# Placing four mixing steps one group later, and giving the operand loads of the merges a pool of their own

## The chip, the cores and the metric

The kernel runs on one core of one Trainium2 chip. Its time is device microseconds of one execution of the whole program; a run before and after are compared by the median of several executions. One execution is taken with the hardware profiler, and every row shown below is from that one. The engines are named as in the profile: PE is TensorE (PEld its weight loads), DVE VectorE, ACT ScalarE, POOL GpSimd, SP the sync engine, which here issues all the DMA transfers.

## The reference

A single layer with two parallel branches: stick-breaking attention, and a pooling branch that works at four window lengths.

```python
WINDOWS = (2, 4, 8, 16)                  # four groups of 256 channels
hs = concat(meta, x)                      # 16 + 1024 tokens of 2048
h = rmsnorm(hs, gain)
q, k, v, g_attn, u, g_pool, m_attn, m_pool = split(h @ w_in)
o_attn = stick_breaking_attention(q, k, v) * silu(g_attn)
pooled[g] = mean of u[g] over the last WINDOWS[g] tokens - u[g]
mixed[g] = pooled[g] @ pool_w[g]          # 256 x 256 for each group
o_pool = mixed * pool_scale * silu(g_pool)
merged = sigmoid(m_attn) * (o_attn @ w_attn_up) + sigmoid(m_pool) * (o_pool @ w_pool_up)
out = rmsnorm(hs + merged @ w_out, final_gain)[meta:]
```

The change touches the mixing of pooled channels (`mixed`) and the beginning of the merges (`o_pool @ w_pool_up`).

## The kernel before

All matrix products are in fp32 with three matmuls for one (`mm3`, L137 to L140): an operand is split into a high part h and a low part l, and h x h, h x l and l x h are added up in PSUM. A split is one activation on ACT (L116, writes the high part) and one subtraction, mostly on DVE, for some weights on POOL (L117, writes the low part). So each matrix that is loaded goes through SP (the load), ACT and DVE or POOL before PE can use it. The weights go through three rings of four buffers: `wr` (as loaded, L124), `wh` and `wl` (split).

The large products are done by block products with fewer multiplications, in stages:

* Up to about 985 us: the norm and the first products of the blocks, whose results go to DRAM.
* Phase 2 (L545 to L883): the rest of the products. `duo` (L572 to L622) computes two columns of blocks of 128 channels with three sub-steps, m5, n4 and p3, each with sixteen weight blocks of 128 by 128 and evacuations on DVE (L592, L594). It runs first for the gates of the pooling groups 0 to 2, then for the pooling (L675 to L714), then for the attention heads one by one (`kv`, `gq`, and two gates of the merges after each).
* The merges (L885 to L977): 32 chunks of 48 matmuls each, sixteen for each of `w_pool_up` ("p") and `w_attn_up` ("a"). A chunk multiplies 128 output channels, for both halves of the tokens.
* The output product and the last norm (L979 on).

The loop over the pooling groups (L675) does four things for group g, one after the other. (1) It loads and splits `pool_w[g]` into `pwh` and `pwl`. (2) It computes the channels u of the group with `duo`. (3) For each of the two 128-channel halves (cc = 1, then 0) it forms the window sums by doubling, one addition on DVE over 1024 tokens for each doubling (L692: one for window 2, four for window 16), subtracts u (L697), and splits the result into `ph` (ACT) and `pl` (DVE). (4) It mixes: 24 matmuls of 128x512 with `pwh`/`pwl` as weights and `ph`/`pl` as moving operands into four PSUM tiles `acc`; each is scaled and gated on DVE (L713) into a tile `st` (two buffers) and stored to DRAM, `d_op` (L714, on SP). For the last group the product of its gate (`silu_duo`, "gp" 3) stands between (3) and (4). `acc` is a ring of four PSUM tiles that `duo` uses as well.

At the start of the merges the operands `d_op` (16 tiles of 128x512) and `d_oa` (16 tiles, from the attention) are loaded back into tiles `ol` (L901; six buffers, within the pool `pm` that holds all else of the merges) and split into the operands x (`op`, `oa`). The first chunk's weights are tied: `tc.issue_after` lets their loads be issued only after the sixth of the first eight operand loads (`behind`). The first two gate tiles (`first`, loads of `d_sp`) are asked for ahead of the operands. The order of the chunks is p0, p8, p1, then a0, a8 and so on in turn.

A scheduler lays out the order of each engine's instructions: it goes by the order in which the program asks for them, and by the time at which it thinks that buffers and operands come free. Each engine then works its own list in order. What a change of code does to those lists is therefore read from the lists themselves.

Of the kernel before, what the change touches and what calls it, by code (L numbers as in the profile page):

```python
# [9 lines left out]
F32 = mybir.dt.float32  # L10
# [5 lines left out]
P = 128  # L16
# [56 lines left out]
def trunk_kernel(  # L73
# [37 lines left out]
    def nm(s):  # L111
        uid[0] += 1
        return f"{s}_{uid[0]}"
# [5 lines left out]
    def load_split(hi, lo, src, eng=None):  # L119
        raw = wp.tile([P, 512], F32, tag="wr", name=nm("wr"), bufs=4)  # L120
        if len(src.shape) == 3:
            c = src.shape[2]
            raw, hi, lo = (t.rearrange("p (k c) -> p k c", c=c) for t in (raw, hi, lo))
        nc.sync.dma_start(raw, src)  # L124
        split(hi, lo, raw, eng)
# [102 lines left out]
    with ExitStack() as actx:  # L228
# [395 lines left out]
        def duo(*args):  # L624
            for call in duo_steps(*args):
                call()
# [10 lines left out]
        with ExitStack() as a0ctx:  # L637
# [33 lines left out]
            for i in (0, 2, 1):  # L671
                for calls in every:
                    calls[i]()

            for g, win in enumerate(WINDOWS):  # L675
                pwh = a0.tile([P, 512], F32R, tag="pwh", name=nm("pwh"), bufs=1)
                pwl = a0.tile([P, 512], F32R, tag="pwl", name=nm("pwl"), bufs=1)
                load_split(pwh, pwl, pool_w[g].rearrange("(c p) d -> p c d", p=P))
                pwh, pwl = (t.rearrange("p (c d) -> p c d", d=256) for t in (pwh, pwl))
                d = named["u", g]  # L680
                us = [tok_tile(a0, "u", F32) for _ in range(2)]
                nc.sync.dma_start(us[0][:, META : META + HALF], d_c[d.n])
                nc.sync.dma_start(us[0][:, :META], d_cm[d.n])
                duo(d, lambda key: half_of(us[key[0]], key[1], META), lambda key, t: None, us[1][:, :META])
                ph, pl = [None] * 2, [None] * 2
                for cc in (1, 0):
                    u = us[cc]
                    cur, lo, sh = u, 0, 1
                    while sh < win:
                        nxt = tok_tile(a0, "s", F32)  # L690
                        lo += sh
                        nc.vector.tensor_tensor(out=nxt[:, lo:], in0=cur[:, lo:], in1=cur[:, lo - sh : TOK - sh], op=ALU.add)  # L692
                        cur, sh = nxt, 2 * sh
                    pool_l = a0.tile([P, SEQ], F32R, tag="pl", name=nm("pl"))
                    pool_h = a0.tile([P, SEQ], F32R, tag="ph", name=nm("ph"))
                    raw = cur[:, META:]
                    nc.vector.scalar_tensor_tensor(out=raw, in0=cur[:, META:], scalar=1.0 / win, in1=u[:, META:], op0=ALU.mult, op1=ALU.subtract)  # L697
                    split(pool_h, pool_l, raw)
                    ph[cc], pl[cc] = pool_h, pool_l
                if g == GROUPS - 1:  # L700
                    sils.append(sil_tiles())
                    silu_duo(a0, named["gp", g], sils[g])
                sil = sils[g]
                for dc in range(2):
                    dd = slice(dc * P, (dc + 1) * P)
                    ch = 2 * g + dc
                    for i in range(2):
                        t = slice(i * 512, (i + 1) * 512)
                        a = acc_tile()
                        for n, cc in enumerate((1, 0)):  # L710
                            mm3(a, pwh[:, cc, dd], pwl[:, cc, dd], ph[cc][:, t], pl[cc][:, t], n == 0, n == 1)
                        st = a0.tile([P, 512], F32, tag="st", name=nm("st"), bufs=2)
                        nc.vector.scalar_tensor_tensor(out=st, in0=a, scalar=psc[:, ch : ch + 1], in1=sil[dc][:, t], op0=ALU.mult, op1=ALU.mult)  # L713
                        nc.sync.dma_start(d_op[ch][:, t], st)  # L714

        with tc.tile_pool(name="a1", bufs=1, side="right", reuse_waits="tile") as a1:
            MK = 64 + META
# [176 lines left out]
        q, jj = divmod(j, QD)  # L894
        split(A[q][0][:, jj], A[q][1][:, jj], src)

    with tc.tile_pool(name="pm", bufs=2, side="right", reuse_waits="tile") as pm:

        def fill(A, j, src):
            raw = pm.tile([P, 512], F32, tag="ol", name=nm("ol"), bufs=6)  # L900
            ins = nc.sync.dma_start(raw, src)  # L901
            put(A, j, raw)
            return ins
# [23 lines left out]
        for n, k in enumerate((("p", 0), ("p", KH), ("p", 1))):  # L927
            order.remove(k)
            order.insert(n, k)
        first = [gate("sp", 6, d_sp, 0, t) for t in range(2)]  # L930
        op, oa = [xquads(0, HALF, xo), xquads(1, HALF, xo)], [xquads(2, HALF), xquads(3, HALF, xc)]
        behind = [fill_up(op[t], d_op, t) for t in range(2)][0]
        sps, ms = {}, {}

        def sums(j):
# [15 lines left out]
        forms = w_forms(pm)  # L951
        for n, (kind, c) in enumerate(order):
            if n in (0, 1):
                fill_up(oa[n], d_oa, n)
            if kind == "p":
                gs = [gate("sp", 6, d_sp, c, t) for t in range(2)] if n else first
                for t, a in up_mm(w_pu, op, c, None if n else behind):
                    nc.vector.tensor_tensor(out=gs[t], in0=a, in1=gs[t], op=ALU.mult)
                sps[c] = gs
            else:  # L960
# [225 lines left out]
```

## Time and profile before

| | us |
|---|---|
| three executions | 2588.91, 2588.54, 2584.05 |
| median | 2588.54 |
| the profiled execution, its own time | 2589.82 |
| its span, first to last instruction | 2588.1 |
| PE busy in the span | 2462.5 (95%) |
| DVE, POOL, ACT busy | 1268.1, 1005.4, 896.8 |

The mean granted clock of PE over the span is 0.982 of full. A matmul of 128x512 at full clock starts 0.23 us after the one ahead of it. In rows of the timeline the columns are the start, the duration, then engine, line, operation, what it writes and reads, and in brackets the idle time ahead of it with what ended it. In rows of waits they are the total, the number of times, and the longest. Matmuls of the mixing are known by their operands `ph`, `pl`; those of the merges by their PSUM tile `accb`.

### The profile page before, as it was taken

The numbers are of one execution on the slowest core, as the hardware profiler recorded it, in microseconds if no ns is written. First come the engines' busy times: TensorE is split into PE (matmuls) and PEld (weight loads), VectorE is DVE, ScalarE is ACT, GpSimd is POOL, SyncE is SP. The second block draws the span as 40 slices with busy tenths as digits, with TensorE's granted clock in tenths as the row PEclk, the third lists the DMA queues.
The fourth block names the chain that finished last, engine by engine and source line by source line (L and its number), as shares of the span: only waits on it lengthen the run. The fifth ranks groups of instructions, "written<-read, shape, count | busy, mean of one in ns | idle before, by whom it ended". The sixth has DMA issues, their size and how long they took to land.

```text
span 2588.1 us, 35874 instructions
## 1 busy us (share of the span) xinstructions
PE 2462.5 (95%) x12680; PEld 2087.6 (81%) x12680; DVE 1268.1 (49%) x2089; ACT 896.8 (35%) x1845; POOL 1005.4 (39%) x898
## 2 busy tenths in 40 slices
PE   6899999999999999899999999999949999989998
PEld 5676778888888887888888888888748888867887
DVE  5442234553333344575676567656652322445556
ACT  6421122222222234224454455545431111144243
POOL 1655555554454544233323333333104545520212
PEclk8999999999999999999999999999979999999999
DMA  5566555665555557435334443443286777675534
GB/s 181 168 208 212 196 195 201 215 232 175 179 184 183 184 179 231 133 115 151 123 118 136 127 126 117 141 126 91 86 280 208 250 237 246 225 248 183 190 124 171
DMA packets 390516, 457.81 MB, mean 177 GB/s; under 512 B 32432, under 2 KB 234544, under 8 KB 389296
## 3 DMA queue, kind: packets, MB, share of 16 engines
q1 hardware_dynamic: 390336, 455.53, 54.7%
q8 instruction: 99, 1.62, 0.3%
q14 instruction: 81, 0.66, 0.1%
HBM read 313.11 MB, written 142.31 MB: 176 GB/s over the span
## 4 chain that ended last, share of the span: by engine, by line
PE 77%; DMA 7%; DVE 6%; POOL 3%; ACT 2%; issue 2%; SPq 0%; DVEq 0%; POOLq 0%; ACTq 0%
PE acc L138 17%; PE acc L140 17%; PE acc L139 17%; PE accb L138 4%; PE accb L139 4%; PE accb L140 4%; POOL r L270 3%; PE accb L1012 2%; PE accb L1011 2%; PE accb L1010 2%; DMA mr<-d_f 2%; DMA raw<-in_w_in_dram 2%; PE tr L764 1%; DVE s L692 1%; DVE x L117 1%
## 5 line engine op out<-in xcount | busy, mean ns | idle before, releaser
L138 PE MATMUL acc<-x,wh 128*128 128x512 f32 (+2 forms) x2736 | 980.1, 359 | 25.2 <-ACT wh L116 16.4
L140 PE MATMUL acc<-x,wl 128*128 128x512 f32 (+2 forms) x2736 | 971.1, 355 | 7.3 <-DVE wl L117 6.0
L139 PE MATMUL acc<-x,wh 128*128 128x512 f32 (+2 forms) x2736 | 968.8, 354 | 0.0
L138 PEld LDWEIGHTS acc<-x,wh 128*128 128x128 f32 x2736 | 519.4, 190 | 97.0 <-ACT wh L116 22.1
L140 PEld LDWEIGHTS acc<-x,wl 128*128 128x128 f32 x2736 | 518.3, 189 | 85.3 <-DVE wl L117 13.3
L139 PEld LDWEIGHTS acc<-x,wh 128*128 128x128 f32 x2736 | 519.4, 190 | 62.7
L116 ACT ACTIVATE wh<-wr 128x512 fp32r<-128x512 f32 x408 | 256.6, 630 | 593.7 <-PE accb L139 235.4
L117 DVE TENSOR_TENSOR wl<-wr,wh 128x512 fp32r<-128x512 f32 x288 | 221.1, 770 | 248.2 <-ACT wh L116 230.0
L117 DVE TENSOR_TENSOR wl<-r,wh 128x512 fp32r<-128x512 f32 x160 | 149.5, 938 | 345.6 <-ACT wh L116 328.5
L117 POOL TENSOR_TENSOR wl<-wr,wh 128x512 fp32r<-128x512 f32 x120 | 166.6, 1388 | 346.0 <-ACT wh L116 289.3
L116 ACT ACTIVATE wh<-r 128x512 fp32r<-128x512 f32 x160 | 100.3, 631 | 474.9 <-POOL r L270 369.6
L270 POOL TENSOR_TENSOR r<-raw,raw 128x512 f32<-128x512 f32 x80 | 111.1, 1388 | 379.2 <-DMA raw<-in_w_in_dram 348.9
L138 PE MATMUL accb<-x,wh 128*128 128x512 f32 x512 | 200.2, 391 | 32.4 <-ACT wh L116 32.4
L270 POOL TENSOR_TENSOR r<-r,raw 128x512 f32<-128x512 f32 x160 | 221.6, 1385 | 12.5 <-DMA raw<-in_w_in_dram 2.5
L139 PE MATMUL accb<-x,wh 128*128 128x512 f32 x512 | 199.9, 390 | 0.0
L140 PE MATMUL accb<-x,wl 128*128 128x512 f32 x512 | 199.7, 390 | 0.0
L1010 PE MATMUL accb<-wh,x 128*128 128x512 f32 x416 | 163.8, 394 | 7.1 <-ACT wh L116 7.0
L1012 PE MATMUL accb<-wl,x 128*128 128x512 f32 x416 | 164.2, 395 | 0.2
L1011 PE MATMUL accb<-wh,x 128*128 128x512 f32 x416 | 162.7, 391 | 0.0
L748 DVE TENSOR_TENSOR_SCAN wt<-wt 128x272 f32<-128x272 f32 (+5 forms) x128 | 107.7, 842 | 110.2 <-POOL wt L743 64.8
L117 DVE TENSOR_TENSOR wl<-raw,wh 128x512 fp32r<-128x512 f32 x136 | 102.6, 765 | 100.9 <-ACT wh L116 100.8
L116 ACT ACTIVATE wh<-raw 128x512 fp32r<-128x512 f32 x160 | 97.6, 624 | 135.2 <-PE acc L139 100.3
(176 smaller groups left out, 3059.5 us busy)
## 6 DMA issues: line engine op xcount, KB each, us to landing
raw<-in_w_in_dram SPq DMA_DIRECT2D x96, 512.0 KB, 5.8
d_r<-r SPq DMA_DIRECT2D x160, 256.0 KB, 2.0
wr<-d_r SPq DMA_DIRECT2D x160, 256.0 KB, 2.9
raw<-in_w_in_dram SPq DMA_DIRECT2D x152, 256.0 KB, 5.3
wr<-in_w_in_dram SPq DMA_DIRECT2D x80, 256.0 KB, 3.0
cw<-in_w_out_dram SPq DMA_DIRECT2D x64, 256.0 KB, 5.1
d_wf<-cw SPq DMA_DIRECT2D x64, 256.0 KB, 2.8
wr<-d_wf SPq DMA_DIRECT2D x64, 256.0 KB, 3.0
```

What stands on the lines that cost most here:

```text
L116: nc.scalar.activation(hi, src, AF.Copy)
L117: (eng or nc.vector).tensor_tensor(out=lo, in0=src, in1=hi.bitcast(F32), op=ALU.subtract)
L138: nc.tensor.matmul(ps, wh, rh, start=first, stop=False, skip_group_check=skip)
L139: nc.tensor.matmul(ps, wh, rl, start=False, stop=False, skip_group_check=skip)
L140: nc.tensor.matmul(ps, wl, rh, start=False, stop=last, skip_group_check=skip)
L270: nc.gpsimd.tensor_tensor(out=t, in0=a, in1=b, op=ALU.add)
L692: nc.vector.tensor_tensor(out=nxt[:, lo:], in0=cur[:, lo:], in1=cur[:, lo - sh : TOK - sh], op=ALU.add)
L748: nc.vector.tensor_tensor_scan(out=rev, data0=rev, data1=rev, initial=wt[:, w : w + 1], op0=ALU.mult, op1=ALU.bypass)
L764: nc.tensor.transpose(tr[:, n, :], bt[:, off : off + P], ident)
L1010: nc.tensor.matmul(a, sh, wh, start=first and j == 0, stop=False, skip_group_check=not first)
L1011: nc.tensor.matmul(a, sl, wh, start=False, stop=False, skip_group_check=not first)
L1012: nc.tensor.matmul(a, sh, wl, start=False, stop=j == KH - 1, skip_group_check=not first)
```

## The change

```diff
--- before.py
+++ after.py
@@ -672,16 +672,37 @@
                 for calls in every:
                     calls[i]()
 
+            mixed = {}
+
+            def mix_weights(g):
+                pw = [a0.tile([P, 512], F32R, tag=f"pw{m}", name=nm("pw"), bufs=1) for m in range(2)]
+                load_split(*pw, pool_w[g].rearrange("(c p) d -> p c d", p=P))
+                return [t.rearrange("p (c d) -> p c d", d=256) for t in pw]
+
+            def mix(g, pwh, pwl):
+                ph, pl = mixed.pop(g)
+                for dc in range(2):
+                    dd = slice(dc * P, (dc + 1) * P)
+                    ch = 2 * g + dc
+                    for i in range(2):
+                        t = slice(i * 512, (i + 1) * 512)
+                        a = acc_tile()
+                        for n, cc in enumerate((1, 0)):
+                            mm3(a, pwh[:, cc, dd], pwl[:, cc, dd], ph[cc][:, t], pl[cc][:, t], n == 0, n == 1)
+                        st = a0.tile([P, 512], F32, tag="st", name=nm("st"), bufs=2)
+                        nc.vector.scalar_tensor_tensor(out=st, in0=a, scalar=psc[:, ch : ch + 1], in1=sils[g][dc][:, t], op0=ALU.mult, op1=ALU.mult)
+                        nc.sync.dma_start(d_op[ch][:, t], st)
+
             for g, win in enumerate(WINDOWS):
-                pwh = a0.tile([P, 512], F32R, tag="pwh", name=nm("pwh"), bufs=1)
-                pwl = a0.tile([P, 512], F32R, tag="pwl", name=nm("pwl"), bufs=1)
-                load_split(pwh, pwl, pool_w[g].rearrange("(c p) d -> p c d", p=P))
-                pwh, pwl = (t.rearrange("p (c d) -> p c d", d=256) for t in (pwh, pwl))
+                if g:
+                    pw = mix_weights(g - 1)
                 d = named["u", g]
                 us = [tok_tile(a0, "u", F32) for _ in range(2)]
                 nc.sync.dma_start(us[0][:, META : META + HALF], d_c[d.n])
                 nc.sync.dma_start(us[0][:, :META], d_cm[d.n])
                 duo(d, lambda key: half_of(us[key[0]], key[1], META), lambda key, t: None, us[1][:, :META])
+                if g:
+                    mix(g - 1, *pw)
                 ph, pl = [None] * 2, [None] * 2
                 for cc in (1, 0):
                     u = us[cc]
@@ -697,21 +718,11 @@
                     nc.vector.scalar_tensor_tensor(out=raw, in0=cur[:, META:], scalar=1.0 / win, in1=u[:, META:], op0=ALU.mult, op1=ALU.subtract)
                     split(pool_h, pool_l, raw)
                     ph[cc], pl[cc] = pool_h, pool_l
-                if g == GROUPS - 1:
-                    sils.append(sil_tiles())
-                    silu_duo(a0, named["gp", g], sils[g])
-                sil = sils[g]
-                for dc in range(2):
-                    dd = slice(dc * P, (dc + 1) * P)
-                    ch = 2 * g + dc
-                    for i in range(2):
-                        t = slice(i * 512, (i + 1) * 512)
-                        a = acc_tile()
-                        for n, cc in enumerate((1, 0)):
-                            mm3(a, pwh[:, cc, dd], pwl[:, cc, dd], ph[cc][:, t], pl[cc][:, t], n == 0, n == 1)
-                        st = a0.tile([P, 512], F32, tag="st", name=nm("st"), bufs=2)
-                        nc.vector.scalar_tensor_tensor(out=st, in0=a, scalar=psc[:, ch : ch + 1], in1=sil[dc][:, t], op0=ALU.mult, op1=ALU.mult)
-                        nc.sync.dma_start(d_op[ch][:, t], st)
+                mixed[g] = ph, pl
+            pw = mix_weights(GROUPS - 1)
+            sils.append(sil_tiles())
+            silu_duo(a0, named["gp", GROUPS - 1], sils[-1])
+            mix(GROUPS - 1, *pw)
 
         with tc.tile_pool(name="a1", bufs=1, side="right", reuse_waits="tile") as a1:
             MK = 64 + META
@@ -894,10 +905,12 @@
         q, jj = divmod(j, QD)
         split(A[q][0][:, jj], A[q][1][:, jj], src)
 
-    with tc.tile_pool(name="pm", bufs=2, side="right", reuse_waits="tile") as pm:
+    with ExitStack() as mctx:
+        po = mctx.enter_context(tc.tile_pool(name="po", bufs=6, side="right", reuse_waits="tile"))
+        pm = mctx.enter_context(tc.tile_pool(name="pm", bufs=2, side="right", reuse_waits="tile"))
 
         def fill(A, j, src):
-            raw = pm.tile([P, 512], F32, tag="ol", name=nm("ol"), bufs=6)
+            raw = po.tile([P, 512], F32, tag="ol", name=nm("ol"))
             ins = nc.sync.dma_start(raw, src)
             put(A, j, raw)
             return ins
@@ -927,9 +940,10 @@
         for n, k in enumerate((("p", 0), ("p", KH), ("p", 1))):
             order.remove(k)
             order.insert(n, k)
-        first = [gate("sp", 6, d_sp, 0, t) for t in range(2)]
-        op, oa = [xquads(0, HALF, xo), xquads(1, HALF, xo)], [xquads(2, HALF), xquads(3, HALF, xc)]
-        behind = [fill_up(op[t], d_op, t) for t in range(2)][0]
+        op, oa = [], []
+        for t in range(2):
+            op.append(xquads(t, HALF, xo))
+            fill_up(op[t], d_op, t)
         sps, ms = {}, {}
 
         def sums(j):
@@ -951,10 +965,11 @@
         forms = w_forms(pm)
         for n, (kind, c) in enumerate(order):
             if n in (0, 1):
+                oa.append(xquads(3, HALF, xc) if n else xquads(2, HALF))
                 fill_up(oa[n], d_oa, n)
             if kind == "p":
-                gs = [gate("sp", 6, d_sp, c, t) for t in range(2)] if n else first
-                for t, a in up_mm(w_pu, op, c, None if n else behind):
+                gs = [gate("sp", 6, d_sp, c, t) for t in range(2)]
+                for t, a in up_mm(w_pu, op, c, None):
                     nc.vector.tensor_tensor(out=gs[t], in0=a, in1=gs[t], op=ALU.mult)
                 sps[c] = gs
             else:
```

In the loop over the groups the mixing (4) of group g is no longer in the turn of its own group: the mixing of group g-1, with the load of its weights, stands after `duo` of group g. The last group's mixing stays where it was, after its gate. `mix_weights` and `mix` hold the old lines, `mixed` keeps `ph` and `pl` in between, and the tiles `pwh`/`pwl` are now `pw0`/`pw1`, named `pw`.

In the merges the tiles `ol` come from a pool `po` of their own, opened ahead of `pm`. The weights of the first chunk are no longer tied to an operand load, the first two gate tiles are asked for in their turn in the loop, and the operand tiles `op` and `oa` are made just ahead of their loads.

What this makes of PE's list shows after u of group 1. Before, the last matmuls of u (into `acc_9468`, with x and wh) are followed by the mixing of the same group 1, whose `ph_9665` was made from that u:

```order
L138 MATMUL acc_9468<-x_1651_8857,wh_9631 128x256
L139 MATMUL acc_9468<-x_1652_8858,wh_9631 128x256
L140 MATMUL acc_9468<-x_1651_8857,wl_9630 128x256
L138 MATMUL acc_9678<-ph_9665,pwh_9453 128x512
L138 MATMUL acc_9688<-ph_9665,pwh_9453 128x512
L138 MATMUL acc_9698<-ph_9665,pwh_9453 128x512
L138 MATMUL acc_9708<-ph_9665,pwh_9453 128x512
L139 MATMUL acc_9678<-pl_9664,pwh_9453 128x512
L140 MATMUL acc_9678<-ph_9665,pwl_9454 128x512
```

After, the same u (now `acc_9422`) is followed by the mixing of group 0, whose `ph_9396` was made one turn earlier:

```order
L138 MATMUL acc_9422<-x_1651_8857,wh_9585 128x256
L139 MATMUL acc_9422<-x_1652_8858,wh_9585 128x256
L140 MATMUL acc_9422<-x_1651_8857,wl_9584 128x256
L138 MATMUL acc_9614<-ph_9396,pw_9407 128x512
L139 MATMUL acc_9614<-pl_9395,pw_9407 128x512
L140 MATMUL acc_9614<-ph_9396,pw_9408 128x512
L138 MATMUL acc_9614<-ph_9403,pw_9407 128x512
```

And ahead of it, where the mixing of group 0 stood, u of group 1 (`acc_9421`) now follows u of group 0 (`acc_9201`) at once:

```order
L138 MATMUL acc_9201<-x_1651_8857,wh_9364 128x256
L139 MATMUL acc_9201<-x_1652_8858,wh_9364 128x256
L140 MATMUL acc_9201<-x_1651_8857,wl_9363 128x256
L138 MATMUL acc_9421<-x_1607_8682,wh_9426 128x256
L139 MATMUL acc_9421<-x_1608_8683,wh_9426 128x256
L140 MATMUL acc_9421<-x_1607_8682,wl_9425 128x256
```

So on PE each mixing has moved behind 144 matmuls of the next group, and the matmuls of a mixing now go tile by tile.

DVE's list around the end of u of group 2. Before, the sums of that group (`s`), the splits `pl`, and behind all of them the evacuations of its own mixing (`st`):

```order
L697 SCALAR_TENSOR_TENSOR s_9929<-s_9929,u_9725 128x1024
L592 TENSOR_TENSOR u_9724<-nu_9730,acc_9732 128x256
L592 TENSOR_TENSOR u_9724<-nu_9730,acc_9733 128x256
L692 TENSOR_TENSOR s_9936<-u_9724 128x1039
L117 TENSOR_TENSOR pl_9931<-s_9929,ph_9932 128x1024
L692 TENSOR_TENSOR s_9938<-s_9936 128x1037
L692 TENSOR_TENSOR s_9940<-s_9938 128x1033
L697 SCALAR_TENSOR_TENSOR s_9940<-s_9940,u_9724 128x1024
L117 TENSOR_TENSOR pl_9942<-s_9940,ph_9943 128x1024
L713 SCALAR_TENSOR_TENSOR st_9954<-acc_9947,psc,sl_8662 128x512
L713 SCALAR_TENSOR_TENSOR st_9964<-acc_9957,psc,sl_8662 128x512
```

After, u of group 2 (`u_9678` and `u_9679`) is pooled in the same place, and the evacuations of the mixing of group 1 stand between its sums:

```order
L718 SCALAR_TENSOR_TENSOR s_9923<-s_9923,u_9679 128x1024
L592 TENSOR_TENSOR u_9678<-nu_9684,acc_9686 128x256
L592 TENSOR_TENSOR u_9678<-nu_9684,acc_9687 128x256
L713 TENSOR_TENSOR s_9930<-u_9678 128x1039
L693 SCALAR_TENSOR_TENSOR st_9886<-acc_9879,psc,sl_8660 128x512
L693 SCALAR_TENSOR_TENSOR st_9896<-acc_9889,psc,sl_8660 128x512
L693 SCALAR_TENSOR_TENSOR st_9906<-acc_9899,psc,sl_8661 128x512
L117 TENSOR_TENSOR pl_9925<-s_9923,ph_9926 128x1024
L693 SCALAR_TENSOR_TENSOR st_9916<-acc_9909,psc,sl_8661 128x512
L713 TENSOR_TENSOR s_9932<-s_9930 128x1037
L117 TENSOR_TENSOR pw_9942<-wr_9943,pw_9941 128x512
```

The evacuations have moved ahead of the second half's sums, and with them their waits for PE and for the stores of `st`.

SP's list at the start of the merges. Before, behind the last stores of phase 2 (L839, with tiles `st`) come the two gate loads and then the operand loads `ol`:

```order
L839 DMA d_sp_119<-st_18726 128x512
L839 DMA d_sp_118<-st_18766 128x512
L923 DMA sp_18842<-d_sp_104 128x512
L923 DMA sp_18844<-d_sp_104 128x512
L901 DMA ol_18862<-d_op_80 128x512
L901 DMA ol_18866<-d_op_81 128x512
```

and the first weights `wr` only behind the last of 24 operand loads:

```order
L901 DMA ol_18950<-d_oa_78 128x512
L901 DMA ol_18954<-d_oa_79 128x512
L124 DMA wr_18960<-in_w_pool_up_dram 128x4x128
L124 DMA wr_18966<-in_w_pool_up_dram 128x4x128
L189 DMA cw_19022<-in_w_out_dram 128x512
```

After, eight weight loads, those of the first four chunks, stand between the last stores (now L850), and the operand loads (now L914) follow without the gates:

```order
L124 DMA wr_19071<-in_w_pool_up_dram 128x4x128
L799 DMA d_oa_79<-st_18641 128x512
L124 DMA wr_19077<-in_w_pool_up_dram 128x4x128
L850 DMA d_sp_119<-st_18685 128x512
L124 DMA wr_19148<-in_w_pool_up_dram 128x4x128
L124 DMA wr_19154<-in_w_pool_up_dram 128x4x128
L850 DMA d_sp_119<-st_18726 128x512
L124 DMA wr_19224<-in_w_attn_up_dram 128x4x128
L124 DMA wr_19230<-in_w_attn_up_dram 128x4x128
L850 DMA d_sp_118<-st_18766 128x512
L914 DMA ol_18849<-d_op_80 128x512
```

The loads of the weights have moved from behind the operand loads to ahead of the last stores of phase 2.

## The prediction

> **What bounds the kernel now.** I read the page first: the rows of busy tenths, then the chain that ended last.
>
> ```profile
> span 2588.1 us, 35874 instructions
> ...
> PE   6899999999999999899999999999949999989998
> ...
> PEclk8999999999999999999999999999979999999999
> ...
> PE 77%; DMA 7%; DVE 6%; POOL 3%; ACT 2%; issue 2%; SPq 0%; DVEq 0%; POOLq 0%; ACTq 0%
> ```
>
> TensorE is busy nine tenths or more nearly everywhere, and 77% of the chain lies on it, so only time in which it waits or runs slowly can be won. A slice is 64.7 us. Two dips lie where the diff works: the seventeenth slice (1035 to 1100 us, the mixing) and the thirtieth (1876 to 1941 us, the start of the merges, with the clock row at 7 as well). Next come TensorE's waits, by what ended them, from 980 to 1200 us and from 1840 to 1960 us:
>
> ```profile
> PE acc L138 <- ACT ph L116: 11.1, 5, 3.7
> PE acc L138 <- ACT wh L116: 5.4, 2, 3.5
> PE acc L139 <- DVE pl L117: 1.5, 3, 0.7
> ```
>
> ```profile
> PE accb L138 <- ACT wh L116: 32.4, 2, 31.1
> ```
>
> The columns are total, times and longest. 11.1 and 1.5 us are waits for the pooled operands ph and pl; the 5.4 us are weights' and stay. At the merges one wait of 31.1 us is for the first split weights, wh. All of this stands on TensorE, so it counts fully.
>
> **The mixing, shifted.** TensorE's timeline from the first mixing matmul of group 0 to the first matmul after the mixing of group 3:
>
> ```profile
> 1052.25 0.39 PE L138 MATMUL acc<-ph,pwh 128*128 128x512 f32 x1
> ...
> 1057.88 1.82 PE L138 MATMUL acc<-ph,pwh 128*128 128x512 f32 x4 [1.97 <-ACT ph L116]
> 1059.50 0.63 PE L139 MATMUL acc<-pl,pwh 128*128 128x512 f32 x1
> 1059.92 0.63 PE L140 MATMUL acc<-ph,pwl 128*128 128x512 f32 x1
> ...
> 1080.68 1.20 PE L138 MATMUL acc<-ph,pwh 128*128 128x512 f32 x4 [0.72 <-ACT ph L116]
> ...
> 1164.45 0.28 PE L138 MATMUL acc<-x,wh 128*128 128x256 f32 x1
> ```
>
> The same stretch by windows (TensorE, weight loads, VectorE, ScalarE, GpSimd busy, then granted clock, DMA share, GB/s): the matmuls of u for group 2, then its pooling and mixing, then those of u for group 3 together with its gate:
>
> ```profile
> 1092.50:1110.00 17.50, 17.50 (x145) 17.43 (x143) 10.05 (x14) 3.87 (x7) 3.59 (x2) 1.00 0.45 139
> 1110.00:1124.20 14.20, 9.20 (x27) 6.47 (x26) 11.18 (x12) 2.80 (x4) 1.78 (x1) 0.76 0.24 76
> 1124.20:1158.10 33.90, 33.90 (x218) 31.07 (x217) 26.57 (x29) 9.75 (x16) 12.04 (x7) 1.00 0.40 123
> ```
>
> The stretch lasts 1164.45 - 1052.25 = 112.2 us. What must be computed in it: three sets of u matmuls at 17.5 us = 52.5; the gate's 72 matmuls, 33.9 - 17.5 = 16.4 us, or 0.228 us each; four mixings of 24 such matmuls, 96 x 0.228 = 21.9. Together 90.8 us, so 21.4 us are lost: 12.6 us idle (11.1 + 1.5), and the rest in matmuls 0.42 us apart instead of 0.228, as the pair at 1059.50 and 1059.92 shows after an idle of 1.97 us (after 0.72 us four take 1.20 instead of 1.82).
>
> After the change u of group 1 follows u of group 0 directly, and each mixing finds its pooling done in the 17.5 us of the next group's u. The last mixing stays behind the gate, which covered its pooling before too. No matmul is added, and the mixing's weights have more time than before. So the whole 21.4 us can go. What is late next is VectorE. For group 2 it needs 10.05 + 11.18 = 21.2 us, pooling and evacuations included, in a period of 17.5 + 24 x 0.228 = 23.0 us. That fits, though in FIFO order with the evacuations of the older mixing between the sums. Those evacuations write st, which has two buffers, so a third one waits for a store that SP issues:
>
> ```profile
> DMA to landing us min/median/max: 2.0/2.5/4.9
> ```
>
> This is the landing of those stores from 1055 to 1166 us. A third evacuation waits for the first one's store, less the time of the evacuation between them (some 0.6 us): 1.9 us by the median landing and 4.3 by the longest, out of VectorE's slack of 23.0 - 21.2 = 1.8 us. That leaves a stall of 0.1 us a group by the median and 2.5 by the longest, and two groups are so tight (beside u of group 3 there is the gate too). The bounds of the remaining stall are thus 0 and 5 us; below 0 is excluded, since full pace is the floor. I take 1.5, nearer to the median landing. The mixing term is **21.4 - 1.5 = 19.9 us less**.
>
> **The start of the merges.** SP's queue, then the first operand splits on ScalarE, the last ones of the pool operand on VectorE, and TensorE:
>
> ```profile
> 1879.23 14.19 SPq L901 DMA_DIRECT2D ol<-d_op  x16
> ...
> 1900.75 0.97 SPq L124 DMA_DIRECT2D wr<-in_w_pool_up_dram  x2
> ...
> 1931.10 1.53 SPq L124 DMA_DIRECT2D wr<-in_w_attn_up_dram  x2
> ```
>
> ```profile
> 1884.22 3.96 ACT L116 ACTIVATE x<-ol 128x512 fp32r<-128x512 f32 x6 [6.40 <-DMA ol<-d_op]
> ```
>
> ```profile
> 1897.67 2.68 DVE L117 TENSOR_TENSOR x<-ol,x 128x512 fp32r<-128x512 f32 x4 [1.01 <-ACT x L116]
> ```
>
> ```profile
> 1876.05 0.39 PE L140 MATMUL acc<-x,wl 128*128 128x512 f32 x1
> 1907.56 0.80 PE L138 MATMUL accb<-x,wh 128*128 128x512 f32 x1 [31.13 <-ACT wh L116]
> ...
> 1921.90 0.50 PE L138 MATMUL accb<-x,wh 128*128 128x512 f32 x1 [1.32 <-ACT wh L116]
> ```
>
> The first weights are issued at 1900.75, behind 24 operand loads, and the first chunk (48 matmuls) starts at 1907.56 although its 16 operand tiles are split by 1897.67 + 2.68 = 1900.35 at the latest (the four in this row hold the last of them, at about 1899). The second chunk starts at 1921.90.
>
> After the change the weights of the first four chunks stand on SP ahead of the last stores of the gates, so they are split when the operands come. The operand loads go out about 0.5 us earlier, because the two gate loads ahead of them on SP go behind. The first chunk then runs as its operands drip in, from about 1885 to 1900: each tile allows three matmuls (0.7 us at full pace, 1.3 us at half), and tiles come about every 0.9 us. Its end is set by the sixteenth tile, split at 1898.5 to 1899.8, plus three matmuls: 1900.0 (1899.2 to 1900.5). The second chunk starts there instead of at 1921.90: 21.9 us less. All loads of operands keep their six buffers, so none of them comes sooner than its predecessor's split allows, before or after.
>
> What is late next is the fifth chunk's weights, the first that find no buffer ahead of time. At 48 x 0.228 = 10.9 us a chunk it is due at 1900 + 3 x 10.9 = 1932.7.
>
> ```profile
> wr<-in_w_attn_up_dram SPq DMA_DIRECT2D x6, 256.0 KB, 6.1
> ```
>
> Such a load takes 6.1 us to land, then some 1.3 us go to the two splits. The row of 1931.10 was their issue before. Three pairs of weight loads have left the queue ahead of it, at 0.97 us a pair by the row of 1900.75: 1928.2 at the latest, so ready by 1935.6 and 2.9 us late. But entries ahead of it also waited for buffers of chunks that now end 21.9 us sooner, so it may be not late at all. Of 0 to 2.9 us I take 1.0, as an estimate. Sum of the merges: **21.9 - 1.0 = 20.9 us less**. From the sixth chunk to the end each engine's order is the same, and TensorE bounds it, so the shift is carried to the end.
>
> **Sum.** 2589.82 (profiled execution) - 19.9 - 20.9 = 2549.0. This execution stands 1.3 us above the median, 2588.54, so the forecast is **2548**. Its own range: both unknown stalls at 0 and the earliest chunk give 2544, both at their upper ends with the latest chunk 2554.
>
> **Rivals.** *The dripping first chunk stays at half pace.* Idle times of 0.3 to 1.2 us between triples of matmuls may keep the granted clock down. Then its 48 matmuls at 0.427 us take 20.5 us from 1884.2, ending at 1904.7 instead of 1900.0: 2553. Against it stands the row at 1080.68, where 0.72 us of idle cost no pace; for it, that the chunk starts cold after 8 us without work. [...]
>
> *VectorE becomes the bound in phase 2.* Its sums run beside GpSimd's splits, which cost time:
>
> ```profile
> 1081.86 2.32 DVE L692 TENSOR_TENSOR s<-u 128x1039 f32<-128x1039 f32 x1
> 1084.21 1.24 DVE L692 TENSOR_TENSOR s<-s 128x1037 f32<-128x1037 f32 x1
> ```
>
> The same kind of sum takes 1.1 us more in the first row. Three such collisions and one late store make about 5 us a group, 15 in all: 2563. [...] For it: only 1.8 us of slack a group. Against it: the group after has the gate's 16.4 us more of matmuls, which takes up delay.
>
> *The merges gain only half.* If the first matmul waits for all sixteen tiles, as one wait on the operand's last buffer would make it, the chunk runs from 1899, ends about 1911.9 with a cold start, and the gain is 10 us: 2559. The order gives each matmul its own tile, so this is unlikely.
>
> *Slower.* If SP, which issues each store only in its turn behind loads that wait themselves, lets each of a group's four evacuations wait the longest landing seen, 4.9 us (19.6 us), VectorE needs 21.2 + 19.6, about 41 us a group, where TensorE needs 23.0. Three groups then lose about 3 x 18 = 54 us, against a gain without that stall of 42.3 (21.4 + 20.9): 2602. It decides from 23.0 + 42.3 / 3 = 37 us a group on. The store row's median of 2.5 us speaks against it.
>
> **How the numbers follow.** A measurement of this kernel can tell about 0.2%, 5 us, from no change. Chances: forecast 0.66, half pace 0.13, VectorE bound 0.11, half the gain 0.06, slower 0.03, no change 0.01 (both parts undone by waits that replace them). All but the last two are faster by over 0.2%: faster 0.96, same 0.01, slower 0.03. The range goes from 2542 (the forecast's 2544 less some scatter, as the runs of before reach 4.5 us under their median) to 2563, where VectorE bounds; outside it lie the last two cases and what exceeds the prices.
>
> **What would show it.** Right: no wait for ph between the first u and the attention, and that stretch about 20 us shorter; at the merges some 8 us of first wait instead of 31.1 and then short ones for x; the second chunk 24 us after the last matmul of phase 2 instead of 45.9. Wrong: TensorE waiting for ph or for acc while VectorE waits for d_op<-st (VectorE bound, or slower); matmuls of the first chunk 0.42 us apart to its end (half pace); its first matmul at 1899 (half the gain); a long wait at the fifth chunk.

## The result, and the profile after

The changed kernel takes **2549.07 us** (median of four executions, 2542.63 to 2552.26) against 2588.72 before (four executions, 2584.05 to 2592.87). The ratio is 0.9844, with a 95% interval of 0.9818 to 0.9870: 1.3 to 1.8% faster. The forecast was 2548, the range 2542 to 2563. A second set of four executions, beside other kernels, gave 2550.45, ratio 0.9859 (0.9845 to 0.9874).

The profiled execution took 2548.13 us. Its page, the same rows as before:

```profile
span 2546.4 us, 35882 instructions
...
PE   6898999999999999999999999999989999999998
...
PEclk8999999999999999999999999999999999999999
...
PE 79%; DMA 6%; DVE 4%; POOL 3%; issue 2%; ACT 1%; SPq 0%; DVEq 0%; POOLq 0%; ACTq 0%
```

The row of PE has lost the 8 at the mixing (its seventeenth digit), and the 4 at the start of the merges is an 8 (the thirtieth, 1846 to 1910 us), with a 9 in the clock row where a 7 was. TensorE's waits from 980 to 1200 us (the total, the times, the longest):

```profile
PE acc L138 <- ACT wh L116: 5.2, 2, 2.8
PE acc L140 <- DVE wl L117: 1.3, 1, 1.3
PE acc L138 <- DVE u L594: 0.6, 1, 0.6
PE acc L138 <- DVE u L592: 0.5, 1, 0.5
PE acc L138 <- DVE st L693: 0.2, 1, 0.2
```

The waits for ph and pl (12.6 us before) are gone; what is left of the mixing are the last four rows, 2.6 us, all for VectorE, which itself waits for the stores (from 1040 to 1170 us):

```profile
DVE st L693 <- DMA d_op<-st: 10.8, 4, 4.0
```

Three of these four waits (2.0, 4.0 and 1.4 us) lie ahead of the attention; the fourth (3.5 us) comes behind its first matmul.

TensorE's waits in the merges (from 1856 to 2100 us), and its timeline there:

```profile
PE accb L138 <- ACT x L116: 8.2, 1, 8.2
PE accb L138 <- ACT wh L116: 4.0, 1, 4.0
```

```profile
1855.35 0.39 PE L140 MATMUL acc<-x,wl 128*128 128x512 f32 x1
1863.90 0.79 PE L138 MATMUL accb<-x,wh 128*128 128x512 f32 x1 [8.16 <-ACT x L116]
...
1869.34 0.39 PE L138 MATMUL accb<-x,wh 128*128 128x512 f32 x1
1869.57 0.39 PE L139 MATMUL accb<-x,wh 128*128 128x512 f32 x1
...
1877.74 0.39 PE L138 MATMUL accb<-x,wh 128*128 128x512 f32 x1
...
1914.65 0.80 PE L138 MATMUL accb<-x,wh 128*128 128x512 f32 x1 [4.00 <-ACT wh L116]
1915.25 0.63 PE L139 MATMUL accb<-x,wh 128*128 128x512 f32 x1
1915.67 0.63 PE L140 MATMUL accb<-x,wl 128*128 128x512 f32 x1
```

The 31.1 us have become 8.2, the second chunk starts 1877.74 - 1855.35 = 22.4 us after the last matmul of phase 2 (45.9 before), and the first chunk is back at full pace, 0.23 us a matmul, from its thirteenth matmul on. But the fifth chunk (1914.65) waits 4.0 us for its weights, and its matmuls then start 0.42 us apart for a while.

**Where the 41.7 us between the two spans come from.** From u of group 1 to the first matmul of the attention before took 112.2 us (counted from the first mixing, in whose place u of group 1 now stands) and after 1144.99 - 1051.17 = 93.8: 18.4 us. From the last matmul of phase 2 to the sixth chunk, behind which the merges run without a wait in both, before took 1965.59 - 1876.05 = 89.5 us and after 1928.31 - 1855.35 = 73.0: 16.6 us. The remaining 6.7 us lie where the two kernels have the same order: 1.1 ahead of this stretch, 1.2 in the attention, 4.4 in the output stage. The experiments have to show whose these are, and what the two parts are worth apart.

### The profile page after: what moved, and what is told of

Its sections match the earlier page's. It is cut to its first block, busy times and chain, and to the rows that moved or that the text cites. A ratio compares the mean times of both kernels' runs of the same rounds, so it can differ in the third digit from the quotient of the medians.

```text
span 2546.4 us, 35882 instructions
## 1 busy us (share of the span) xinstructions
PE 2454.0 (96%) x12680; PEld 2087.1 (82%) x12680; DVE 1268.5 (50%) x2089; ACT 896.1 (35%) x1845; POOL 1005.8 (39%) x898
## 4 chain that ended last, share of the span: by engine, by line
PE 79%; DMA 6%; DVE 4%; POOL 3%; issue 2%; ACT 1%; SPq 0%; DVEq 0%; POOLq 0%; ACTq 0%
PE acc L138 17%; PE acc L139 17%; PE acc L140 17%; PE accb L138 4%; PE accb L140 4%; PE accb L139 4%; PE accb L1027 3%; PE accb L1025 3%; PE accb L1026 3%; POOL r L270 3%; DMA raw<-in_w_in_dram 2%; PE tr L775 1%; DMA mr<-d_f 1%; DVE bt L760 1%; PE z L139 1%
## 5 line engine op out<-in xcount | busy, mean ns | idle before, releaser
L138 PEld LDWEIGHTS acc<-x,wh 128*128 128x128 f32 x2736 | 519.9, 190 | 98.7 <-ACT wh L116 21.9
```

The lines of the kernel that those rows point to most:

```text
L138: nc.tensor.matmul(ps, wh, rh, start=first, stop=False, skip_group_check=skip)
```

## The experiments

Times are medians of four executions (of seven or eight for before), all ratios are against before on the same chip in the same session. There were three sessions. In the first (each part alone, the tiles zz alone, the combinations put off and bunched) before gave 2585.18 us, in the second (the tie, the tiles ol in pm, the combinations spread out, and the kernel after that) 2586.84, in the third (the last three) 2589.11. Differences under about 5 us between kernels of different sessions mean nothing.

### Each part by itself

The first two kernels have one part of the change each: the loop of the groups as changed and the merges as before, and the other way round.

> The kernel of before with the mixing steps moved and nothing else; the merges are as before. Theory (the two parts are separate, each gives what its own stretch shows in the changed kernel): from u of group 1 to the first matmul of the attention 93.8 us as in the changed kernel, where before took 112.2, so 18.4 us less; the wait of about 31 us for the first weights of the merges is still there; 2570 (2567 to 2573). Rival (the moved steps' gain is given back at the merges, whose start some DMA or store sets): last matmul of phase 2 some 19 us earlier, but the wait at the merges longer by 5 us or more; 2575 to 2589.

2568.2 us, ratio 0.9924 (0.9899 to 0.9949): 17.0 less than before beside it. The stretch takes 93.0 us. The waits of the merges:

```profile
PE accb L138 <- ACT wh L116: 31.5, 2, 30.0
```

The long wait is 30.0 us, not longer: nothing of the mixing's gain is given back there. The theory holds, the rival falls.

> The kernel of before with the merges' part alone: operand loads in a pool of their own, first weights untied. Theory: the second chunk starts 22 to 23 us after the last matmul of phase 2 instead of 45.9, and the fifth chunk waits about 4 us for its weights and then runs at half pace for a while, so that from the sixth chunk on 16.6 us are won; the output stage, whose waits fell by 4.4 us in the changed kernel, belongs to this part as well: 2588.7 - 21.0 = 2568 (2565 to 2570). Rival (those 4.4 us are chance of one execution or belong to the moved mixing): 2572 (2570 to 2574). Second rival (the merges gain only because phase 2 ends otherwise): no more than 10 us, above 2578.

2567.12 us, ratio 0.9928 (0.9904 to 0.9952): 18.1 less than before beside it. TensorE's waits from 1850 to 2100 us and in the output stage:

```profile
PE accb L138 <- ACT x L116: 8.4, 1, 8.4
PE accb L138 <- ACT wh L116: 2.2, 1, 2.2
```

```profile
PE accb L1014 <- ACT wh L116: 6.0, 2, 4.9
```

From the last matmul of phase 2 to the sixth chunk it took 70.9 us, 18.7 less than before, where the changed kernel gained 16.6; the wait at the fifth chunk is shorter here (2.2 instead of 4.0). The output stage's wait for weights is 6.0 us here, where it was 7.0 before and 5.1 after. In the other kernels of this study it ranged from 4.0 (the shift alone, whose merges are those of before) to 8.2 us. The whole stage, from its first matmul to the end, took 328.8 us in before and 324.4 in the changed kernel, but 328.0 in a second profiled execution of the same changed kernel (the repeat below), and 323.5 to 331.6 over all kernels. So the 4.4 us are taken for scatter between executions and for neither part's gain. The time lies at the number expected by the first theory, but on a before of 2585.2 rather than the 2588.7 that both were reckoned from; 18.1 us less lies between their 21.0 and 16.6 and doesn't decide. The two parts by themselves are worth 17.0 + 18.1 = 35.1 us, the two stretches of the trace together 18.4 + 16.6 = 35.0. The whole change gained 39.7 us in the first set of executions and 38.7 in the second; the intervals of the two parts, some 6 us each way, leave that difference open.

### Which edit of the merges does it

The tie alone was put back on the changed kernel:

```diff
-            fill_up(op[t], d_op, t)
+            sixth = fill_up(op[t], d_op, t)
+            behind = sixth if t == 0 else behind
...
-                for t, a in up_mm(w_pu, op, c, None):
+                for t, a in up_mm(w_pu, op, c, None if n else behind):
```

> The changed kernel with the first chunk's weights tied again to the sixth operand load; the pool of their own, the gates and the mixing stay as changed. Theory (the tie alone put those weights behind 24 operand loads on SP): the first wait of the merges is 30 us again, the second chunk starts 45 to 46 us after the last matmul of phase 2, and the time is that of the moved mixing alone, 2568 (2565 to 2571). Rival (the pool of its own or the gates' place carries a part): a wait of 20 us or less, below 2562.

2569.03 us, ratio 0.9923 (0.9901 to 0.9946). SP's timeline, and TensorE's wait:

```profile
1860.48 13.90 SPq L914 DMA_DIRECT2D ol<-d_op  x16
1874.73 6.46 SPq L914 DMA_DIRECT2D ol<-d_oa  x8
1881.25 0.90 SPq L936 DMA_DIRECT2D sp<-d_sp  x2
1882.19 0.98 SPq L124 DMA_DIRECT2D wr<-in_w_pool_up_dram  x2
```

```profile
PE accb L138 <- ACT wh L116: 32.6, 2, 30.9
```

The tie names the sixth load, but puts the weights behind 24 of them and two gate loads, and the whole gain of the merges is gone. The theory holds. Then the other way round, the tiles ol back in the pool pm:

```diff
-        po = mctx.enter_context(tc.tile_pool(name="po", bufs=6, side="right", reuse_waits="tile"))
...
-            raw = po.tile([P, 512], F32, tag="ol", name=nm("ol"))
+            raw = pm.tile([P, 512], F32, tag="ol", name=nm("ol"), bufs=6)
```

> The changed kernel with the operand tiles ol back in the pool pm (six buffers as before), the weights untied. Theory (the pool of its own changes nothing that ends last): SP's list is the same but for names, the first wait of the merges is about 8 us, 2547 to 2551. Rival (in pm the tiles ol lie where late tiles of phase 2 lie, so their loads start later): the operand loads start later than 2.7 us after the last matmul of phase 2, where they start in the changed kernel, and the first wait is 10 us or more.

2549.09 us, ratio 0.9858 (0.9839 to 0.9878). The first wait is 8.1 us, and the operand loads start 2.7 us after the last matmul of phase 2 as in the changed kernel. The pool of their own is worth nothing, and taking off the tie does the work. What then remains of this part is the place of the first two gate loads, which was not tried by itself: the operand loads start 2.7 us after the last matmul of phase 2 instead of 3.2, so by that it gives about 0.5 us at most. The title names the pool and four mixing steps; by these runs it is the tie that counts, and three mixing steps moved, the last having stayed behind its gate.

### What TensorE still loses in the mixing

The evacuations of the second half of each mixing were put into the tiles zz, of which two are free there:

```diff
-                        st = a0.tile([P, 512], F32, tag="st", name=nm("st"), bufs=2)
+                        st = a0.tile([P, 512], F32, tag=("st", "zz")[dc], name=nm("st"), bufs=2)
```

> The changed kernel, with the evacuations of the second half of each mixing in the tiles zz (two buffers that are free there), so that four evacuations need not wait for a store. Theory (VectorE's waits for the stores, 10.8 us in four times in this stretch, make the 3.0 us that TensorE still loses there): those waits under 2 us, TensorE's stretch from u of group 1 to the attention 91 to 92 us instead of 93.8, time 2 to 2.5 us less, 2546.5. Rival (VectorE is full anyway, the waits only fill its slack): the stretch stays at 93.5 to 94 us, 2549.

2545.2 us, ratio 0.9840 (0.9810 to 0.9869), not to be told from the changed kernel by the time. The trace tells: VectorE's waits for d_op<-st are gone, and the stretch has not one wait of TensorE's. Its window from the first matmul of u of group 1 to the first of the attention, in the changed kernel and here (length, then TensorE's busy time):

```profile
1051.17:1144.99 93.82, 91.47 (x603) 83.92 (x601) 77.06 (x89) 26.77 (x42) 28.61 (x18) 1.00 0.47 146
```

```profile
1053.90:1144.50 90.60, 90.60 (x602) 84.00 (x601) 77.47 (x90) 27.05 (x42) 29.24 (x17) 1.00 0.50 159
```

90.6 us is what the matmuls need, busy from end to end; VectorE is as busy as ever (77.5 us), so it is not full, it was held up by the stores. The stretch came to the same 90.6 us in all four kernels with these tiles. In the seven profiled executions with the changed loop and two buffers (six kernels, the changed one twice) it lasted 91.7 to 96.0 us, that is 1.1 to 5.4 us over it, 3.0 in the mean. The longest single wait of VectorE's for a store ahead of the attention goes with it: where it was 4.2 or 4.3 us, 5.4 us were lost; where it was 2.1 to 2.7 us, 1.1 to 2.4.

### What makes the fifth chunk wait

SP's timeline of the changed kernel ahead of the fifth chunk's weights:

```profile
1896.45 2.68 SPq L194 DMA_DIRECT2D d_wf<-cw  x4
1899.18 1.51 SPq L936 DMA_DIRECT2D sp<-d_sp  x2
1902.05 1.76 SPq L189 DMA_DIRECT2D cw<-in_w_out_dram  x4
1903.85 2.92 SPq L936 DMA_DIRECT2D sa<-d_sa  x4
1907.27 1.06 SPq L124 DMA_DIRECT2D wr<-in_w_attn_up_dram  x2
```

cw and d_wf belong to another job: combinations of the output weights, made on GpSimd in steps that the loop of the chunks hands out. I put them off until the fourth chunk was done:

```diff
-            for _ in range(2 if n % 2 else 1):
+            for _ in range(0 if n < 4 else 3 if n < 8 else 2 if n % 2 else 1):
```

> The changed kernel, with the output weights' combinations (loads cw, stores d_wf) begun after the fourth chunk of the merges and caught up by the eighth, so that SP has none of them ahead of the fifth chunk's weights. Theory (those weights came late, issued at 1907.27, because they stood in SP's queue behind eight loads and four stores that wait for one another): the fifth chunk's wait of 4.0 us is gone, and with it the 2.8 us of half pace behind it, 6.8 us less in the merges, 2542 (2540 to 2545). Rival (the transfers themselves are late, the DMA engines are 0.8 to 1.0 busy there): a wait of 3 us or more stays, 2547 to 2549.

2559.86 us, ratio 0.9898 (0.9873 to 0.9923), 10.8 more than the changed kernel's 2549.07 of an earlier session: the expected time was missed by 18 us. The fifth chunk no longer waits, as the theory said. But TensorE waits later, at the tenth and the twelfth chunk (from 1960 to 2010 us):

```profile
1969.05 0.50 PE L138 MATMUL accb<-x,wh 128*128 128x512 f32 x1 [1.63 <-ACT wh L116]
...
1977.95 0.80 PE L138 MATMUL accb<-x,wh 128*128 128x512 f32 x1 [2.95 <-ACT wh L116]
...
2003.74 0.79 PE L138 MATMUL accb<-x,wh 128*128 128x512 f32 x1 [4.85 <-ACT wh L116]
```

SP's timeline shows what the weights of the tenth chunk stood behind:

```profile
1960.30 1.01 SPq L124 DMA_DIRECT2D wr<-in_w_attn_up_dram  x1
1967.58 5.95 SPq L194 DMA_DIRECT2D d_wf<-cw  x4
1973.58 0.42 SPq L981 DMA_DIRECT2D d_f<-sa  x1
1974.10 0.41 SPq L124 DMA_DIRECT2D wr<-in_w_attn_up_dram  x1
```

Between the two halves of this chunk's weights lie 13.8 us, most of them SP's turn at stores d_wf that were not ready, since GpSimd wrote their tiles from 1966.27 us on. From the last matmul of phase 2 to the output stage this kernel took 11.1 us more than the changed one (377.8 against 366.7), although the fifth chunk no longer waited. The expectation had looked at the one wait only. Made up singly, one step more at every fourth chunk, the same delay should do no harm:

```diff
-            for _ in range(2 if n % 2 else 1):
+            for _ in range(0 if n < 4 else (2 if n % 2 else 1) + (n % 4 == 0)):
```

> The changed kernel with the output weights' combinations begun after the fourth chunk, and the six steps left out made up singly, one more at every fourth chunk, where the run before made them up within four chunks. Theory (it was the bunched catching up that made chunks 9 to 11 wait): neither the fifth chunk nor any behind it waits more than 1 us, 6.8 us less than the changed kernel, 2542 (2540 to 2545). Rival (any combination begun late stands in the way of later weights on SP, since its stores wait for GpSimd): some chunk from the sixth on waits 2 us or more, 2547 or more.

(The chunks 9 to 11 of this text are counted from 0: the tenth to the twelfth.)

2545.98 us, ratio 0.9838 (0.9823 to 0.9852). The weights of the fifth chunk are issued 38 us after the last matmul of phase 2 instead of 52, and from 1850 to 2100 us the first wait (8.2 us) is TensorE's only one. In the trace the theory holds: from the last matmul of phase 2 to the sixth chunk it took 66.2 us instead of 73.0, 6.8 less. The time moved by 3 to 4.5 us (3.1 against the kernel beside it with the tiles ol in pm, which differs from the changed one by a pool worth nothing); the intervals leave 6.8 open. The next kernel leaves out only the third and fourth chunks' steps and has the tiles zz as well:

```diff
-            for _ in range(2 if n % 2 else 1):
+            for _ in range(0 if n in (2, 3) else (2 if n % 2 else 1) + (n in (6, 10, 14))):
```

> The changed kernel with two edits: the evacuations of the second half of each mixing in the tiles zz, and only the third and fourth chunks without a step of the combinations (three steps, made up at the seventh, eleventh and fifteenth). Theory: no idle of TensorE in the mixing stretch (3 us less), and the fifth chunk's weights go out 3 us earlier, so it waits 1 us or less (3.0 to 6.8 us less with the half pace behind it): 2541 (2538 to 2544). Rival (waits come back at later chunks): 2546 or more.

2540.18 us, ratio 0.9817 (0.9802 to 0.9831), as expected: no wait in the mixing, none at the fifth chunk.

### The two mends together, and an earlier start of the merges

Three kernels ran side by side: the changed one again; the one with the tiles zz and the combinations spread out; and a third with two edits more, which take the last stores and the fourth chunk's weights out of SP's way to the operand loads:

```diff
-                    nc.sync.dma_start(half_of(to[d.i + key[0]], key[1]), t)
+                    (nc.sync if step is not None else nc.scalar).dma_start(half_of(to[d.i + key[0]], key[1]), t)
...
-            fill_up(op[t], d_op, t)
+            sixth = fill_up(op[t], d_op, t)
+            behind = sixth if t == 0 else behind
...
-                for t, a in up_mm(w_au, oa, c, None):
+                for t, a in up_mm(w_au, oa, c, behind if n == 3 else None):
```

> The changed kernel itself, beside the two that follow on the same chip: 2549 (2546 to 2552), the fifth chunk's wait 2 to 4 us, 2 to 5.5 us lost in the mixing stretch.

2550.45 us; the fifth chunk waits 3.9 us, and the mixing stretch loses 1.1 us, less than I had expected.

> The changed kernel with both mends that worked by themselves: evacuations of the second half of each mixing in the tiles zz, and the combinations begun after the fourth chunk and made up singly. Theory: no idle in the mixing stretch, no wait at the fifth chunk or behind it: 3 us and 5 to 6.8 us less, 2540 (2538 to 2543). Rival (they gave what they gave by chance): 2545 or more.

2541.36 us, ratio 0.9820 (0.9804 to 0.9837): 9.1 us under the changed kernel beside it, without a wait in the mixing or behind the first chunk.

> The kernel of the run before this one, with two more edits: the last gate's stores are issued from ScalarE's queue, and the fourth chunk's weights are tied to the sixth operand load, so that SP comes to the operand loads with only six weight loads ahead of them. Theory (the first operand of the merges comes late because its load stands behind two weight loads and a last store on SP, each of which waits for the end of phase 2): the operand loads start 2 to 5 us ahead of the last matmul of phase 2 instead of 2.7 us behind it, the first wait falls from 8.2 us to 1 to 4, and 5 us are won: 2535 (2533 to 2539). Rival (the tiles where the loads or splits go are still in use until phase 2 ends): the first wait stays at 7 us or more, 2540. Second rival (the fourth chunk's weights are now late): a wait of 2 us or more there, 2540 or more.

**2535.5 us**, ratio 0.9801 (0.9785 to 0.9818), 15 us under the changed kernel, the fastest of the study. SP's and TensorE's timelines:

```profile
1845.45 0.37 SPq L124 DMA_DIRECT2D wr<-in_w_pool_up_dram  x1
1845.91 15.29 SPq L914 DMA_DIRECT2D ol<-d_op  x16
```

```profile
1849.14 0.39 PE L140 MATMUL acc<-x,wl 128*128 128x512 f32 x1
...
1852.00 0.49 PE L138 MATMUL accb<-x,wh 128*128 128x512 f32 x1 [2.47 <-ACT x L116]
1852.73 0.50 PE L139 MATMUL accb<-x,wh 128*128 128x512 f32 x1 [0.23 <-DVE x L117]
1853.06 0.56 PE L140 MATMUL accb<-x,wl 128*128 128x512 f32 x1
1853.42 0.63 PE L138 MATMUL accb<-x,wh 128*128 128x512 f32 x1
```

The operand loads start 3.2 us ahead of the last matmul of phase 2 instead of 2.7 behind it, and the first wait falls from 8.5 us in the kernel beside it to 2.5; the time is 5.9 us less than that kernel's. No chunk behind the first waits for weights, so both rivals fall. What each of the two edits gives apart was not run.

## Why the prediction was right, and where its terms were off

The mechanism was right in both places: the waits named for removal went, nothing took their place at full size, and no rival came. The sum was right partly by luck, since two terms were too large, together by 5.8 us, and 6.7 us came from where none was forecast.

* **The mixing, 19.9 us forecast, 18.4 in the profiled execution.** The loss of 21.4 us was sized right: 112.2 us less the 90.6 that the stretch takes without any wait is 21.6. The remaining stall was put at 0 to 5 us with 1.5 taken; it is 1.1 to 5.4 us over seven executions, 3.0 in the mean. Its cause was the one named, VectorE waiting with a third evacuation for a store: with four buffers it is zero. The 1.5 came too low because one of the three waits in the stretch, 4.0 us, was near the 4.3 reckoned from the longest landing; the other two, 2.0 and 1.4, were near the 1.9 of the median.
* **The start of the merges, 21.9 us forecast, 23.5 measured** (45.9 less 22.4). The first wait was forecast at 8 us and is 8.2. The first chunk did run at half pace (0.42 us a matmul, granted clock 0.50 from 1863.90 to 1868.50 us), but for its first twelve matmuls only; from then on its operands were there in time, with no idle recorded between its matmuls.
* **The fifth chunk, 1.0 us forecast (0 to 2.9), 6.9 measured.** This is the step that was mis-sized. From the fourth chunk's start to the sixth's are 1928.31 - 1899.61 = 28.7 us, where two chunks take 21.8. Of the 6.9 us 4.0 are the wait. The latest case of the prediction came true almost to the number: counted from the last matmul of phase 2, the weights were issued at 51.9 us (52.1 in that case) and the chunk began at 59.3 (59.5), but it was due at 55.3 instead of 56.6, since the chunks ahead of it had started earlier than forecast. I had taken 1.0 because entries ahead of the weights on SP might move forward with the chunks. They didn't, because among them stand the combinations of the output weights, whose loads and stores wait for one another; with them out of the way the weights go out at 38 us and the wait is zero. The other 2.9 us are matmuls at half pace behind the wait (0.42 us apart, granted clock 0.50 from 1914.65 to 1920 us), a cost that the prediction used in the mixing and left out here.
* **From the sixth chunk to the end: no change forecast, 4.4 us less measured**, and 2.3 us elsewhere. The second profiled execution of the changed kernel had 3.6 of the 4.4 back, and the output stage's wait for weights varies between 4.0 and 8.2 us over all kernels, whichever parts they hold, so this is taken for scatter; what sets it in a given execution was not looked into.

The rivals, by the same runs: *half pace throughout the first chunk* falls by its own sign, since the pace is 0.23 us from 1869.34 on. But the idle of 0.3 to 1.2 us between triples that it was built on didn't come either: while the first matmuls started 0.42 us apart or more, the operands got ahead. *VectorE as the bound* named the right engine and the right stores, but 3 us instead of 15: VectorE is held up, not full (busy 77.1 of the stretch's 93.8 us). The collisions it was sized from stand in the trace of before: the sum at 1081.86 us (2.32 us) ran beside a split on GpSimd from 1081.23 to 1083.08 us, the one at 1084.21 us (1.24 us) beside none. *Half the gain* falls, the first matmul starts with the first tile. *Slower* would have needed 37 us a group, 111 for three; three groups, the gate and the last mixing together take 93.8.

## What to carry to other kernels

Look at what stands ahead of a load in its queue, related or not: here one tie to "the sixth load" put the weights behind 24 loads (first wait 30.9 us instead of 8.2), and steps of an unrelated job in the same queue cost the fifth chunk 6.9 us. When a wait is removed, follow the queue on to the next load without a buffer ahead of time, and price its wait with the slow matmuls that follow it (2.1 to 3.0 us on top at the fifth chunk). Work that is put off is best made up thinly: bunched, it cost 10.8 us more than the changed kernel here, singly 3.1 less than the kernel beside it.

## What the runs showed of the hardware

The longer waits of TensorE in these streams of 128x512 matmuls cost more than their length, since the matmuls behind them started 0.42 us apart instead of 0.23 for a while. The granted clock was 0.50 over such a stretch (before, 1908.0 to 1911.5 us, behind the wait of 31.13) and 1.00 once they were 0.23 apart (1912 to 1921 us). In the mixing and the merges of all the traces every wait of 2.17 us or more had such matmuls behind it. Single waits of 1.32, 1.51 and 1.74 us at the second chunk, and of 1.9 us in the mixing of the kernel with that part alone, had none: the chunk behind the 1.32 us took 11.05 us from its start to the next one's, 0.17 over a chunk at full pace. In between it went both ways. Behind the wait of 1.97 us in the mixing of before the matmuls were slow, four of them taking 1.82 us; behind the same wait in the kernel with the merges' part alone they kept full pace:

```profile
1056.96 1.20 PE L138 MATMUL acc<-ph,pwh 128*128 128x512 f32 x4 [1.97 <-ACT ph L116]
```

Shorter waits close together did it too: 1.63 and then 1.08 us, within 2 us of each other at the tenth chunk of the bunched kernel, were followed by slow matmuls. At the fifth chunk, where two chunks take 21.76 us without a wait, five executions show the price:

| wait, us | time over 21.76 us, us | paid on top of the wait, us |
|---|---|---|
| 2.17 | 4.4 | 2.2 |
| 2.89 | 5.0 | 2.1 |
| 2.98 | 5.1 | 2.1 |
| 3.90 | 6.9 | 3.0 |
| 4.00 | 6.9 | 2.9 |

In the fastest kernel idles of 0.20 and 0.22 us in the first chunk, at 1861.84 and 1862.57 us, left the pace at 0.23 to 0.24 us.
